# Hybrid convolution/RWKV-7/MLA block on one core: pace of the first three triangular inversions and the distance between their blocks' loads and merges

## The chip, the core and the metric

The kernel runs on one core of a Trainium2 chip: TensorE (PE) multiplies into PSUM, VectorE (DVE) and ScalarE (ACT) work on SBUF and PSUM, GpSimd (POOL) and SyncE (SP) issue most of the DMAs. Each engine takes its own instructions strictly in order and waits on semaphores of the others. The metric is device microseconds (us) from launch to end; lower is better.

## The reference, cut to what matters

Two layers on 1024 latent and 256 context tokens of width 1024. The first layer mixes a short convolution with an RWKV-7 recurrence in 8 heads of 64, run forward and backward; the second is multi-head attention with low-rank keys and queries.

```python
def rwkv7_scan(r, decay, k, v, a_vec, b_vec, s0, reverse):
    def step(S, inp):
        r_t, w_t, k_t, v_t, a_t, b_t = inp
        sa = jnp.einsum('bhij,bhj->bhi', S, a_t)
        S = S * w_t[:, :, None, :] + sa[..., None] * b_t[:, :, None, :] + v_t[..., None] * k_t[:, :, None, :]
        return S, jnp.einsum('bhij,bhj->bhi', S, r_t)
    ...
def even_mixer(...):
    p_all = (h_ctx @ w_in, h_lat @ w_in)
    streams = [rwkv_prep(p[..., A_COLS:A_COLS + RWKV_SHIFT_COLS], mu, k_k) for p in p_all]
    for d, reverse in enumerate((False, True)):
        ...
            decay, k_dir, b_vec = rwkv_direction(k, wl, al, kk, w0[d], w2[d], a0[d], a2[d], k_a)
            y, state = rwkv7_scan(r, decay, k_dir, v, -kk, b_vec, state, reverse)
    ...
```

The kernel does the recurrence in 20 chunks of 64 tokens. Inside a chunk the dependence of each step on those before it is a unit triangular 64x64 matrix, and its inverse is needed for every chunk, head and direction before the scan over chunks can start.

## The kernel before

**The stage.** The change lies in the first layer, in the stretch from about 180 to 720 us of the span. There four kinds of work run interleaved:

- the *chain*: the projections of the first layer (`project`, line 444, 24 matmuls of 128x512 or 128x256 for each part of the 1280 tokens), with what follows them (convolution, gates, shifts);
- the *units*: head pairs j = 0..3 times five groups q of four chunks. A unit (`unit`) makes decays, operands and, for each direction d, the chunk products (`chunks`: line 702 multiplies into PSUM, line 705 masks them on DVE into `M`, whose parts SP sends to HBM, among them the triangular blocks in `g2_d`);
- the *inversion* `invert(j)` of head pair j, which starts when the five units of j are done, so it runs beside the units of j + 1. The inversion of j = 3 has no units left beside it and has an order of its own;
- slices of the second layer's modulation vectors (`ada`, lines 168 to 181).

**The inversion, in steps.** `invert` is a generator, and each `yield` ends a step. Step 1 loads the 32x32 diagonal blocks of both directions (`BL`, line 753, eight DMAs). Steps 2 to 31 are the substitution on DVE (lines 760 and 762, `tm` and `BL`, two instructions a step). Step 32 copies the transposed blocks (`BT`, line 767) and writes both to HBM (`bi_d`, `bt_d`, lines 768 and 769). Then, for each direction d, `blocks(d)` loads them back in the layout that PE wants: `NQ` (line 782, the off-diagonal block from `g2_d`), `X` (line 783, from `bt_d`) and `W` (line 785, from `bi_d`). Some steps pass with nothing in them, and then come the *merges*: two half products of `NQ` and `X` (line 799, 20 instructions of 32x32 each, copied by ACT into the free rows of `NQ` at line 802) and two half products of `NQ` and `W` (line 809, copied by ACT into `W` at line 812), one half a step. The last step of a direction sends `W` to HBM (line 817). For j < 3 all these DMAs are issued by POOL, for j = 3 by SP. `X` and `NQ` have one buffer each, so the loads of d = 1 wait for the merges of d = 0.

**What sets the order.** Only PE's order is the one in which the code is written (`manual_schedule(engines={ET.PE})`); the order of DVE, ACT, POOL and SP is made by the framework's scheduler from priorities and its own estimates. After each of the four parts of a unit (a *quarter*) the code calls `step(rate)`, which advances the chain by `rate` steps and the running inversion by `INV` steps. So `INV` and the empty steps decide after which quarter, and so at which place among PE's instructions, a merge stands. A unit has four quarters, a head pair 20. What is left of an inversion after 20 quarters is written at once (`advance(inv, 99)`).

Of the kernel before, what the change touches and what calls it, by code (L numbers as in the profile page):

```python
# [51 lines left out]
def build(ctx, tc, I, out, dbg=None):  # L52
# [464 lines left out]
    with ExitStack() as c1:  # L517
# [92 lines left out]
                ready.add(j)  # L610
            yield

        RATE, INV, TAIL = ((1.25, 1.75, 1.65, 1.55), (2.2, 0.7, 1.5, 1.4), (1.5, 1.1, 1.3, 2.1), (1.7, 1.5, 0.8, 1.5)), 2.5, (0.5, 1.2)
        INVM = {ET.PE, ET.DVE}
        PAUSE = (3, 0)
        cs = ExitStack()
# [118 lines left out]
        def merge(j):  # L735
            turn[0] += 1
            if j == 3 and turn[0] % 2:
                t = psa.tile([P, 2, 2 * P], F32, tag="A", name="m").rearrange("p a b -> p (a b)")
            elif turn[0] % 2:
                t = psm.tile([P, 512], F32, tag="m", name="m")  # L740
            else:
                t = psb.tile([P, 512], F32, tag="b", name="m")
            return t[:, 0:320].rearrange("p (u t) -> p u t", t=32)

        def invert(j):

            eng = G if j < 3 else SY
            BL = vp.tile([4 * NCH, 2, 32, 32], F32, tag="vA", name="BL")
            for d in range(2):
                for h in range(2):  # L750
                    for b in range(2):
                        p0, r0 = (2 * d + h) * NCH, b * 32
                        eng.dma_start(out=BL[p0:p0 + NCH, b], in_=g2_d[d][:, h, r0:r0 + 32, j, r0:r0 + 32])
            tm = vp.tile([4 * NCH, 32 * 32], F32, tag="vB", name="tm")
            yield
            for q in range(1, 31):
                m = 31 - q
                tgt = BL[:, :, 0:q, q + 1:32]
                tv = tm[:, 0:2 * q * m].rearrange("p (b k i) -> p b k i", b=2, i=m)
                V.tensor_tensor(tv, BL[:, :, q:q + 1, q + 1:32].broadcast_to([4 * NCH, 2, q, m]),  # L760
                                BL[:, :, 0:q, q:q + 1].broadcast_to([4 * NCH, 2, q, m]), op=ALU.mult)
                V.tensor_tensor(tgt, tgt, tv, op=ALU.add)
                yield
            for b in range(2):
                G.memset(BL[:, b].rearrange("p a b -> p (a b)")[:, 0:1024:33], 1.0)
            BT = vp.tile([4 * NCH, 32, 32], F32, tag="vB", name="BT")
            V.tensor_copy(BT, BL[:, 0].rearrange("p s t -> p t s"))
            eng.dma_start(out=bi_d[j].rearrange("d h u b s t -> (d h u) b s t"), in_=BL)
            eng.dma_start(out=bt_d[j].rearrange("d h u s t -> (d h u) s t"), in_=BT)
            yield  # L770
            rows = [(slice(h * 64, h * 64 + 32), slice(h * 64 + 32, h * 64 + 64)) for h in range(2)]
            halves = (slice(0, 10), slice(10, 20))

            def blocks(d):
                W = vp.tile([P, NCH, C], F32, tag=("vA", "vB")[d], name="W")
                if d and j == 3:

                    X, NQ = (vp2.tile([P, NCH, 32], F32, name=n) for n in ("X", "NQ"))
                else:
                    X, NQ = (vp.tile([P, NCH, 32], F32, tag=t, name=t) for t in ("X", "NQ"))  # L780
                for h, (rl, rh) in enumerate(rows):
                    eng.dma_start(out=NQ[rl], in_=g2_d[d][:, h, 0:32, j, 32:64].rearrange("u s t -> s u t"))
                    eng.dma_start(out=X[rl], in_=bt_d[j][d, h].rearrange("u s t -> s u t"))
                    for b, rb in enumerate((rl, rh)):
                        eng.dma_start(out=W[rb, :, b * 32:b * 32 + 32], in_=bi_d[j][d, h, :, b].rearrange("u s t -> s u t"))
                    G.memset(W[rh, :, 0:32], 0.0)
                return W, X, NQ

            ahead = [blocks(d) for d in range(2)] if j == 3 else []
            for d in range(2):  # L790
                W, X, NQ = ahead[d] if ahead else blocks(d)
                for _ in range((6, 3)[d] if j < 3 else PAUSE[d]):
                    yield
                for i, us in enumerate(halves):
                    ps = merge(j)

                    for u in range(10):
                        for rl, rh in rows:
                            TE.matmul(ps[rh, u, :], NQ[rl, us.start + u, :], X[rl, us.start + u, :], start=True, stop=True,
                                      tile_position=(rl.start, rh.start))  # L800
                    for rl, rh in rows:
                        S.copy(NQ[rh, us], ps[rh])
                    if i or j < 3:
                        yield
                for i, us in enumerate(halves):
                    ps = merge(j)
                    for u in range(10):
                        for rl, rh in rows:
                            TE.matmul(ps[rl, u, :], NQ[rh, us.start + u, :], W[rh, us.start + u, 32:64], start=True, stop=True,
                                      tile_position=(rh.start, rl.start))  # L810
                    for rl, rh in rows:
                        S.copy(W[rl, us, 32:64], ps[rl])
                    if j < 3:
                        yield
                if j < 3:
                    for h in range(2):
                        eng.dma_start(out=g1_d[d].rearrange("c p j h x w -> p c j h x w")[hs[h], :, j, h, 3], in_=W[hs[h]])
                else:
                    last_w.append(W)
                yield  # L820
# [50 lines left out]
        for n, (j, q) in enumerate(uo):  # L871
            decays, operands, chunks, bonus = us[n]
            after = us[n + 1]
            if q == 4:
                need(j + 1)
            if q == 2 and j < 3:
                load_w2(j + 1)
            if q == 4 and j < 3:
                split_w2()
            if after:  # L880
                load_x(*uo[n + 1])
            operands(0)
            step(RATE[j][0])
            operands(1)
            if after:
                after[0](0)
            step(RATE[j][1])
            chunks(0)
            if after:
                after[0](1)  # L890
            step(RATE[j][2])
            chunks(1)
            bonus()
            step(RATE[j][3])
            if q == 4:
                advance(inv, 99)
                inv = invert(j)
# [836 lines left out]
```

## Time and profile before

| | us |
|---|---|
| median of 3 runs | 1842.94 |
| lowest, highest | 1842.92, 1848.52 |
| the profiled execution, its own time | 1844.97 |
| span of the profiled execution | 1843.2 |

The span runs from the first to the last instruction of the profiled execution; the rest of its time lies around it. The rows further down come from that one execution. A timeline row gives start, duration, engine, line, operation and tiles, with the idle time of the engine before it and what ended it in brackets; one matmul instruction of the program can leave two records (the products of 32x32 blocks do: 20 instructions, 40 records).

### The profile page before, as it was taken

To read this page: it belongs to the slowest core of one execution; us is meant where nothing else is said; L and a number is where in the kernel's file an instruction comes from. 1 tells how busy PE (TensorE), PEld (TensorE's weight loads), DVE (VectorE), ACT (ScalarE), POOL (GpSimd) and SP (SyncE) were. 2 spreads that over 40 slices of the span, in tenths; PEclk is the share of its full clock that TensorE was granted. 3 is DMA by queue.
4 is the path that set the end of the run, shared out by engine and by line. 5 is a ranking of instruction groups with operands and counts; after the bars stand their busy time and mean duration, and the time that the engine had idled before them with its cause. 6 is when DMAs were issued, how large, how long until landed. Compare 5 with 4: busy or idle time off the path is not lost.

```text
span 1843.2 us, 36929 instructions
## 1 busy us (share of the span) xinstructions
PE 1699.0 (92%) x14352; PEld 1468.0 (80%) x14352; DVE 1206.3 (65%) x2705; ACT 920.1 (50%) x2333; POOL 199.8 (11%) x231
## 2 busy tenths in 40 slices
PE   4999999999999789875899999989999999999999
PEld 3778887878788678775899877878888888888787
DVE  5747579569669283546488563377786886877822
ACT  5747446565544214555244432276666666666610
POOL 1200010320310200100333100000010010010000
PEclk9999999999999989998999999999999999999999
DMA  9067896997987847998544321210010010001242
GB/s 341 26 189 210 224 217 173 282 243 205 247 206 183 190 148 221 325 325 289 166 145 147 101 69 57 88 31 15 18 40 15 22 35 15 21 18 44 95 143 97
DMA packets 243551, 259.37 MB, mean 141 GB/s; under 512 B 67696, under 2 KB 210416, under 8 KB 236912
## 3 DMA queue, kind: packets, MB, share of 16 engines
q1 hardware_dynamic: 188928, 197.39, 35.7%
q10 hardware_dynamic: 48304, 43.52, 8.2%
q0 software_dynamic: 6144, 16.10, 3.8%
q8 instruction: 113, 1.85, 0.4%
q14 instruction: 62, 0.51, 0.1%
HBM read 164.90 MB, written 92.01 MB: 139 GB/s over the span
## 4 chain that ended last, share of the span: by engine, by line
PE 32%; DVE 12%; ACT 5%; issue 1%; DMA 1%; POOL 0%; SPq 0%; ACTq 0%; DVEq 0%; POOLq 0%
PE p L268 8%; PE s_ps L1498 5%; PE o L268 5%; PE o L1191 3%; PE po L1537 3%; PE pk L268 3%; DVE mx L1501 2%; DVE pL L148 2%; PE pT L1525 2%; ACT jk L1448 1%; PE r_ps L1498 1%; ACT p L1510 1%; ACT pH L147 1%; DMA ro<-oz_d 1%; PE pq L268 1%
## 5 line engine op out<-in xcount | busy, mean ns | idle before, releaser
L444 PE MATMUL p<-h0H,wh 128*128 128x512 f32 x744 | 276.4, 372 | 8.8 <-DVE th L458 8.8
L444 PE MATMUL p<-h0H,wl 128*128 128x512 f32 x744 | 267.3, 359 | 0.0
L444 PE MATMUL p<-h0L,wh 128*128 128x512 f32 x744 | 267.1, 359 | 0.0
L444 PEld LDWEIGHTS p<-h0H,wh 128*128 128x128 f32 x744 | 141.9, 191 | 32.3 <-DVE th L458 9.0
L444 PEld LDWEIGHTS p<-h0H,wl 128*128 128x128 f32 x744 | 141.7, 190 | 22.1
L444 PEld LDWEIGHTS p<-h0L,wh 128*128 128x128 f32 x744 | 142.0, 191 | 19.3
L147 ACT CAST pH<-pT 128x512 fp32r<-128x512 f32 x160 | 94.2, 589 | 75.3 <-PE pT L1525 73.4
L148 DVE TENSOR_TENSOR pL<-pT,pH 128x512 fp32r<-128x512 f32 x160 | 109.7, 686 | 30.7 <-ACT pH L147 29.6
L1498 PE MATMUL s_ps<-kH,q 128*128 128x512 f32 x256 | 108.2, 423 | 0.0
L1525 PE MATMUL pT<-cst,p 128*128 128x128 f32 x640 | 98.1, 275 | 10.1 <-DVE mx L1507 3.5
L1501 DVE TENSOR_REDUCE mx<-s_ps 128x1 f32<-128x512 f32 x128 | 87.7, 685 | 22.6 <-PE s_ps L1498 22.1
L1537 PE MATMUL po<-pL,vH 128*128 128x256 f32 x320 | 93.0, 291 | 6.1 <-DVE pL L148 5.3
L1537 PE MATMUL po<-pH,vH 128*128 128x256 f32 x320 | 95.9, 300 | 0.1
L1191 PE MATMUL o<-mh,woH 128*128 128x256 f32 x320 | 92.1, 288 | 1.2 <-DVE y L1082 1.2
L1525 PEld LDWEIGHTS pT<-cst,p 128*128 128x128 f32 x640 | 74.0, 140 | 23.2 <-DVE pL L148 6.3
L1191 PE MATMUL o<-ml,woH 128*128 128x256 f32 x320 | 90.4, 283 | 0.3 <-DVE ml L148 0.3
L1537 PE MATMUL po<-pH,vL 128*128 128x256 f32 x320 | 90.3, 282 | 0.0
L1191 PE MATMUL o<-mh,woL 128*128 128x256 f32 x320 | 90.3, 282 | 0.0
L1510 ACT ACTIVATE p<-s_ps,mx 128x512 f32<-128x512 f32 x128 | 87.6, 692 | 0.1
L1498 PE MATMUL s_ps<-kr,q 128*128 128x512 f32 x256 | 80.6, 396 | 0.2 <-DVE q L1483 0.2
L268 PE MATMUL p<-h1H,w1h 128*128 128x512 f32 x200 | 79.6, 398 | 0.7 <-ACT acc L1292 0.7
L268 PE MATMUL p<-h1H,w1l 128*128 128x512 f32 x200 | 78.0, 390 | 0.0
(346 smaller groups left out, 4584.9 us busy)
## 6 DMA issues: line engine op xcount, KB each, us to landing
G<-g_d SPq DMA_DIRECT2D x40, 1024.0 KB, 8.0
adaw<-in_ada_w_dram ACTq DMA_DIRECT2D x32, 512.0 KB, 5.2
wr<-in_w_in_dram ACTq DMA_DIRECT2D x31, 512.0 KB, 4.1
g_d<-M SPq DMA_DIRECT2D x80, 192.0 KB, 4.4
x<-rkv_d ACTq DMA_DIRECT2D x20, 512.0 KB, 4.6
g_d<-AR SPq DMA_DIRECT2D x80, 128.0 KB, 3.5
g_d<-M SPq DMA_DIRECT2D x80, 128.0 KB, 4.7
adaw<-in_ada_w_dram SPq DMA_DIRECT2D x8, 1024.0 KB, 13.5
```

The lines of the kernel that those rows point to most:

```text
L147: S.copy(H, x)
L148: eng.tensor_tensor(L, x, f(H), op=ALU.subtract)
L268: TE.matmul(ps, w(kt), x(kt), start=q == 0, stop=q == 3 * n - 1)
L444: TE.matmul(ps[:, :n1 - n0], w[:, kt, :], h[:, kt, n0:n1], start=kt + e == 0, stop=kt + e == KT + 1)
L1191: TE.matmul(ps[m // 2][:, m % 2], w[m][:, 4 * e + kt, :], y[:, kt, :], start=e + m % 2 + kt + i == 0, stop=e + m % 2 + kt + i == 7)
L1448: S.activation(jk[:, :b - a], raw[:, i, a:b], AF.Square, accum_out=ss[:, i, e:e + 1])
L1498: TE.matmul(s, x, y[:, n0:n1], start=e == 0, stop=e == 4)
L1501: V.tensor_reduce(mxs[i][:, b:b + 1], s, axis=mybir.AxisListType.X, op=ALU.max)
L1510: S.activation(pt[:, n0:n1], s_ps[i][e - 1] if e else r_ps[:, i, :], AF.Exp, bias=mx[:, 4:5], accum_out=mx[:, 5 + e:6 + e])
L1525: TE.transpose(ps[:, e, i * P:(i + 1) * P], pts[h, n, i][:, (2 * k + e) * P:(2 * k + e + 1) * P], ident)
L1537: TE.matmul(o, a[:, 2 * k + e, :], b[:, e, :], start=k + e + q_ == 0, stop=k + e + q_ == 7)
```

## The change

Two numbers change. Empty steps between the loads and the merges of the first three inversions: nine and five for the two directions instead of six and three. Steps of the inversion a quarter: 2.9 instead of 2.5. The number of instructions of the kernel's work is the same.

```diff
-        RATE, INV, TAIL = ((1.25, 1.75, 1.65, 1.55), (2.2, 0.7, 1.5, 1.4), (1.5, 1.1, 1.3, 2.1), (1.7, 1.5, 0.8, 1.5)), 2.5, (0.5, 1.2)
+        RATE, INV, TAIL = ((1.25, 1.75, 1.65, 1.55), (2.2, 0.7, 1.5, 1.4), (1.5, 1.1, 1.3, 2.1), (1.7, 1.5, 0.8, 1.5)), 2.9, (0.5, 1.2)
...
-                for _ in range((6, 3)[d] if j < 3 else PAUSE[d]):
+                for _ in range((9, 5)[d] if j < 3 else PAUSE[d]):
                     yield
```

By the count of steps, in quarters after the inversion's start:

| step | before | now |
|---|---|---|
| `BT` copied and written | 13 | 11 |
| loads for d = 0 | 14 | 12 |
| first products (line 799), d = 0 | 16 | 15 |
| second products (line 809), first half, d = 0 | 17 | 15 |
| loads for d = 1 | 18 | 16 |
| first products, d = 1, first and second half | 19, 20 | 18, 18 |
| second products, d = 1 | 20 | 19 |
| last step | 21 | 20 |

Where the merges of the second inversion (j = 1) for d = 0 stand among PE's instructions, before (a chunk product of the units at line 702 stands behind the slice at line 176, and the first products come 24 projection matmuls and one slice later):

```order
L444 MATMUL p<-h0H,wl 128x512
L176 MATMUL ada_pt_5084<-cst,adae 128x2
L702 MATMUL A<-AR,BK 128x128 x8
L709 MATMUL b<-cst,BK 128x128 x4
L727 MATMUL b<-x,cst 128x256
```

and now:

```order
L444 MATMUL p<-h0H,wl 128x512
L176 MATMUL ada_pt_5084<-cst,adae 128x2
L799 MATMUL m<-X,NQ 32x32 x40
L809 MATMUL m<-W,NQ 32x32 x20
L702 MATMUL A<-AR,BK 128x128 x8
L709 MATMUL b<-cst,BK 128x128 x4
L727 MATMUL b<-x,cst 128x256
```

Both halves of the first products and one half of the second have moved ahead of the chunk product. The first (j = 0) and the third inversion (j = 2) have the same three rows at the same kind of place, ahead of the second chunk product of the fourth unit.

DVE at the end of the same inversion, before (`BT` is the 652nd of its instructions):

```order
L760 TENSOR_TENSOR tm<-BL 80x60
L682 TENSOR_TENSOR bk<-bk,x 128x4x64
L762 TENSOR_TENSOR BL<-BL,tm 80x2x30
L685 TENSOR_TENSOR BK<-bk,t_4779 128x4x64
L767 COPY BT<-BL 80x1024
L686 TENSOR_TENSOR BK<-bk,t_4779 128x4x64
```

and now:

```order
L760 TENSOR_TENSOR tm<-BL 80x60
L685 TENSOR_TENSOR BK<-bk,t_4787 128x4x64
L762 TENSOR_TENSOR BL<-BL,tm 80x2x30
L686 TENSOR_TENSOR BK<-bk,t_4787 128x4x64
L767 COPY BT<-BL 80x1024
L178 TENSOR_TENSOR ada_109<-ada_pt_4928,vec 128x2
```

Here the copy of `BT` has moved back by one instruction of the units (line 686). In the third inversion it has moved ahead of three (lines 679, 680 and 681), in the first ahead of thirteen.

PE around the last chunk product of the last unit of j = 3, before (the merges are those of the third inversion, d = 1):

```order
L799 MATMUL m<-X,NQ 32x32 x20
L702 MATMUL A<-AR,BK 128x128 x8
L709 MATMUL b<-cst,BK 128x128 x4
L727 MATMUL b<-x,cst 128x256
L444 MATMUL p<-h0H,wh 128x512
```

and now:

```order
L809 MATMUL m<-W,NQ 32x32 x40
L702 MATMUL A<-AR,BK 128x128 x8
L709 MATMUL b<-cst,BK 128x128 x4
L727 MATMUL b<-x,cst 128x256
L444 MATMUL p<-h0H,wh 128x512
```

Before, the other half of the first products and both second products stood twelve projection matmuls behind this chunk product; now all merges stand ahead of it.

## Rows read from the trace of the kernel before

**Rows 1.** The page: busy time of the engines, then PE in forty slices of the span.

```profile
PE 1699.0 (92%) x14352; PEld 1468.0 (80%) x14352; DVE 1206.3 (65%) x2705; ACT 920.1 (50%) x2333; POOL 199.8 (11%) x231
...
PE   4999999999999789875899999989999999999999
```

**Rows 2.** PE's waits from 180 to 720 us: total, times, longest.

```profile
PE p L444 <- DVE th L458: 8.8, 1, 8.8
...
PE m L809 <- ACT NQ L802: 0.4, 2, 0.2
```

**Rows 3.** Timeline of PE: first products that waited, inversions one to three.

```profile
376.14 0.54 PE L799 MATMUL m<-X,NQ 32*32 32x32 f32 x22 [0.51 <-DMA NQ<-g_d]
...
502.30 0.81 PE L799 MATMUL m<-X,NQ 32*32 32x32 f32 x38 [2.11 <-DMA NQ<-g_d]
...
602.36 0.24 PE L799 MATMUL m<-X,NQ 32*32 32x32 f32 x2 [0.37 <-DMA X<-bt_d]
603.54 1.45 PE L799 MATMUL m<-X,NQ 32*32 32x32 f32 x78 [0.94 <-DMA X<-bt_d]
...
622.26 0.22 PE L799 MATMUL m<-X,NQ 32*32 32x32 f32 x2 [2.62 <-DMA NQ<-g_d]
625.57 1.24 PE L799 MATMUL m<-X,NQ 32*32 32x32 f32 x38 [3.09 <-DMA X<-bt_d]
```

**Rows 4.** Timeline of PE: the chunk products ahead of which the merges now stand.

```profile
340.00 1.16 PE L702 MATMUL A<-AR,BK 64*128 64x128 f32 x16
...
473.68 1.16 PE L702 MATMUL A<-AR,BK 64*128 64x128 f32 x16
...
593.64 1.75 PE L702 MATMUL A<-AR,BK 64*128 64x128 f32 x16 [0.76 <-DVE M L705]
```

**Rows 5.** Busy time of PE, PEld, DVE, ACT, POOL; clock, DMA: second and third substitution.

```profile
407.00:461.70 54.70, 53.61 (x377) 44.26 (x377) 53.82 (x112) 26.11 (x62) 0.23 (x2) 1.00 0.79 221
536.00:588.60 52.60, 52.33 (x342) 44.22 (x342) 51.58 (x113) 20.92 (x51) 0.23 (x2) 1.00 0.70 171
```

**Rows 6.** Timeline of DVE: two of the thirteen instructions, and the copies of `BT`.

```profile
321.64 0.47 DVE L562 SCALAR_TENSOR_TENSOR ea<-ea,dv,eb 128x256 f32<-128x256 f32 x1
...
330.64 0.42 DVE L685 TENSOR_TENSOR BK<-bk,t 128x256 f32<-128x256 f32 x1
330.98 1.11 DVE L767 COPY BT<-BL 80x1024 f32<-80x1024 f32 x1
...
461.75 1.13 DVE L767 COPY BT<-BL 80x1024 f32<-80x1024 f32 x1
...
588.61 1.06 DVE L767 COPY BT<-BL 80x1024 f32<-80x1024 f32 x1
```

**Rows 7.** Line 783 in the second inversion: duration, first and last start; issue to landing.

```profile
L783 POOL DMA_DIRECT2D X<-bt_d x2: 682/688/694, 469.6 to 471.6; - x2
...
DMA to landing us min/median/max: 6.8/6.8/6.8
```

**Rows 8.** Line 783's issue-to-landing times over all inversions.

```profile
DMA to landing us min/median/max: 2.6/3.6/6.8
```

**Rows 9.** The end of the units: PE, DVE and PE, from their timelines.

```profile
626.74 2.08 PE L702 MATMUL A<-AR,BK 64*128 64x128 f32 x16
...
649.82 0.22 DVE L760 TENSOR_TENSOR tm<-BL 80x60 f32<-80x60 f32 x1 [18.65 <-DMA X<-v_d]
...
650.94 0.80 PE L444 MATMUL p<-h0H,wh 128*128 128x512 f32 x1 [8.75 <-DVE th L458]
```

**Rows 10.** Stretches, columns as in rows 5: three at the lower clock, one after a wait.

```profile
351.40:358.20 6.80, 6.80 (x84) 6.56 (x76) 0.00 (x0) 1.73 (x5) 3.33 (x5) 0.50 1.03 292
...
500.00:524.00 24.00, 21.89 (x283) 18.57 (x283) 10.75 (x23) 11.09 (x27) 9.79 (x12) 1.00 0.98 245
...
624.40:631.30 6.90, 5.73 (x62) 5.17 (x63) 1.71 (x3) 1.42 (x3) 0.00 (x0) 0.51 0.85 200
...
645.00:655.20 10.20, 4.26 (x10) 3.39 (x11) 5.04 (x15) 0.00 (x0) 0.00 (x0) 0.50 0.83 221
```

## The prediction, on record before the changed kernel ran

> **What bounds the kernel now.** First the page: PE is busy 92% of the span, and most of its forty slices show 9 or more [rows 1], so an edit counts where it makes PE wait. Then PE's waits in the stage of the change, 180 to 720 us: the longest single one is 8.8 us for DVE at line 458 [rows 2]. Then the timeline of PE at line 799, the first products of the merges: six waits for loads, 0.51 in the first inversion, 2.11 in the second, 0.37, 0.94, 2.62 and 3.09 in the third, 9.6 us in all [rows 3]. These are what a longer distance between loads and merges can take away. Against them stand the places to which the merges move [rows 4], and whether their data can be there by then, which DVE decides: during the substitution it is busy 53.8 of 54.7 us in the second inversion and 51.6 of 52.6 in the third [rows 5].
>
> **The change part by part.**
>
> *The pace, 2.9 for 2.5.* By the count of steps `BT` is written two quarters sooner. But the count orders PE alone. DVE takes the substitution between the units' instructions in an order of its own, and it is full [rows 5]: its order puts `BT` behind one more instruction of the units in the second inversion, ahead of three in the third, ahead of thirteen in the first. An instruction of those costs some 0.42 us less 0.08 of overlap. So `BT` comes 0.4 us later in the second, 1.0 sooner in the third; in the first the thirteen, from 321.64 to 330.64, make 6.8 us sooner [rows 6]. It is not two quarters: from `BT` to `BT`, 461.75 to 588.61, are 20 quarters, 6.3 us each, so two would be 12.7 us.
>
> *From `BT` to `X`.* In the second inversion `BT` is done at 462.88 [rows 6]; the loads of `X` are issued at 469.6 and 471.6 and land 6.8 us later, at 476.4 and 478.4 [rows 7], 13.5 and 15.5 us behind `BT`. In the third `BT` is done at 589.67 and the products start when `X` lands, at 603.54 [rows 3, 6]: 13.9 us.
>
> *Second inversion, d = 0.* The first products now stand ahead of the chunk product that started at 473.68 [rows 4]. `X` lands between 476.4 and 478.4, plus 0.4. The wait is 2.7 to 5.1 us; I take 4.1, near the middle.
>
> *Third inversion, d = 0.* PE reached the chunk product at 593.64 - 0.76 = 592.88 and waited 0.76 for DVE [rows 4]. Now it meets the first products there, whose `X` lands at 603.54 - 1.0 = 602.5: a wait of 9.7, of which 0.76 was there already. 8.9 more, 7.9 to 9.9 with a microsecond for the DMAs either way.
>
> *First inversion, d = 0.* `BT` done at 332.09 - 6.8 = 325.3, `X` 13.9 to 15.5 later, at 339.2 to 340.8, against PE at 340.00 [rows 4]. The last load of `W` follows `X`'s second by two issues of 0.69 [rows 7], as long as the first products take (1.45 us [rows 3]). Together 0 to 1.6; I take 0.8.
>
> *Second products directly behind the first, at three places.* They need ACT's copies of the first half. The nearest row is 0.2 us at most, where this happened before [rows 2]; three times, 0.6. If ACT is in something longer, 1.5. What stands behind a waiting merge on PE is the chunk product, and behind the copies on ACT the units' other evictions, which wait for the same PE work; I add nothing for them.
>
> *The waits that were.* For d = 1 the loads are issued two quarters ahead of the first products instead of one, some 6 us more than the 0.51, 2.11 and 2.62 + 3.09 us that they were late. These go, and 0.37 + 0.94 of the third inversion are replaced by the wait above: -9.6. In the third inversion the merges of d = 0 are themselves so late that `NQ` may still come late: 0 to 2.6, as before; I take 1.0.
>
> *Merges that pass the last chunk product.* Before, one half of the first products and both second products of the third inversion, d = 1, stood behind it. Now they stand ahead: 0.7 + 1.5 us of the shape in rows 3, 2.2. They cost nothing on PE as such. But from that chunk product (626.74) runs the chain to the last inversion: mask, SP's writes, SP's loads of `BL`, first substitution at 649.82, and line 458 behind it, for which PE then stood 8.75 us and went on at 650.94 [rows 9]. That wait swallows nothing, since its end moves with the chunk product. What follows (the rest of the projections, the last merges, the scan) moves with it.
>
> *The clock.* Three stretches of 6.8 to 10.2 us stand at 1.2 instead of 2.4 GHz. PE is busy in them for 6.80, 5.73 and 4.26 us, and loses half of that: 3.4, 2.9, 2.1. The second lies behind the 2.62 and 3.09 us waits, the third in the 8.75 us one; after the 2.11 us wait the clock stayed at 1.00 [rows 9, 10]. The second should go: -2.9. The new waits of 4.1 and 9.7 us should bring one each: 2.0 (0 to 3.4) and 2.1 (as behind the 8.75). Sum 1.2, from -2.9 to 4.5.
>
> **Sum.** 4.1 + 8.9 + 0.8 + 0.6 - 9.6 + 1.0 + 2.2 + 1.2 = 9.2 us. On the profiled execution's own 1844.97 that is 1854.2. The median of the runs shown lies 2.0 below it, so I predict 1852. With all terms at their ends the sum goes from about 0.7 to 17.8, that is 1843.6 to 1860.7 against the median.
>
> **The rivals.**
>
> *The loads land sooner.* Over all inversions `X` took from 2.6 us [rows 8]. With 2.6 instead of 6.8 in the second inversion its wait is gone with the clock's 2.0; a load about 1.0 sooner takes as much off the third: 9.2 - 4.1 - 2.0 - 1.0 = 2.1, some 1845, no change to be measured. For it: the DMAs will be in other company. Against it: the path from `BT` to `X` was 13.5 to 15.5 us in the second and 13.9 in the third.
>
> The Trainium skill, page "DMA: Bandwidth & Descriptors", section "Anatomy of one DMA — SWDGE (gpsimd) path", says that a DMA from GpSimd takes about 2.0 us plus its bytes by 436 GB/s; for a load of 80 KB that is 2.2 us, by my estimate. With such times for writes and loads the second inversion would not wait at all and the third some 6 us less, and the sum would be about -4, some 1839. The trace does not agree: `X` took 6.8 us [rows 7].
>
> *The last inversion does not move.* If the first substitution at 649.82 hangs on a transfer that has nothing to do with the last chunk product, PE's delay (9.2 - 2.2 = 7.0) is swallowed in its 8.75 us wait: no change, 1843. For it: the row names a load of `X` from `v_d` as what came last [rows 9]. Against it: `BL` needs the last chunk's blocks, and SP issues that load behind those of `BL`, so both come with the chunk.
>
> *The substitution really ends two quarters sooner.* It is the other side. If DVE gave the inversion its place by the count, `X` would come 12.7 us sooner, ahead of PE in the second and third inversion. Then no merge of d = 0 waits; 9.6 and the clock's 2.9 are saved, 2.2 is paid: -10.3, about 1833. It decides from a lead of 9.7 us in the third inversion. Against it: rows 5, and the order of DVE's instructions, which is the order in which they run. This is also how the change would do what its numbers say. I see no slack on DVE for it.
>
> **How the numbers follow.** About 0.3% (5.5 us) can be told from no change. The forecast has 0.68, the sooner loads 0.12, the last inversion that stays 0.11, the sooner substitution 0.09. Slower by over 0.3%: 0.68, nearly all of the forecast, and a little more for loads that land later than I have them: 0.69. Within: 0.22. Faster: 0.09. The range from 1843 to 1861 takes in the ends of the sum and the two cases without a change, and leaves out the sooner substitution and what lies beyond the ends.
>
> **What will show it.** In the changed kernel's timeline of PE: at line 799 a wait for `X` of about 4 us in the second inversion (near 475) and of 9 to 10 in the third (near 597), and none over 1 us for d = 1 but perhaps in the third. `BT` within 1.5 us of 461.75 and of 588.61, shifted by what PE has lost by then, and near 324 in the first. Line 809 directly behind line 799 with 0.2 to 0.5 us. The wait for line 458 longer than 8.75 us by about 2, and ending near 660. A stretch at 1.2 GHz at each long wait, and none behind d = 1 of the third. I am wrong if `BT` in the third inversion comes more than 5 us before 588, if PE's wait there is under 5 us, or if the first substitution of the last inversion stays near 650.

## Result and profile of the changed kernel

| | before | after |
|---|---|---|
| median, us (runs) | 1845.73 (4) | 1878.22 (4) |
| lowest, highest | 1842.92, 1852.95 | 1870.61, 1881.44 |
| profiled execution, us | 1844.97 | 1870.61 |
| its span | 1843.2 | 1868.8 |

The change makes the kernel slower: ratio 1.0161, 95% interval 1.0131 to 1.0192, some 30 us (the two medians lie 32.5 apart). The prediction had the direction, but 9 us, and its range ended at 1861. The profiled execution of after is the fastest of its four, so its trace shows 26 of the 30 us.

The page of after, busy time and PE in forty slices (answers to [rows 1]): PE's share fell by a point, and the slice with the first inversion's merges, 327 to 374 us, shows 8 where 9 stood.

```profile
PE 1704.9 (91%) x14352; PEld 1473.1 (79%) x14352; DVE 1206.5 (65%) x2705; ACT 918.2 (49%) x2333; POOL 200.6 (11%) x231
...
PE   4999999899899779777799999989999999999999
```

PE's waits in after, from 180 to 745 us: what was waited for, total, times, longest (answers to [rows 2]). The waits for `NQ` are gone; in their place stand `X`, a longer wait for line 458, and others that the prediction did not have or had smaller: at lines 653, 809 and 799 for ACT, at line 168 for the weights of the slices (`adaw`).

```profile
PE m L799 <- DMA X<-bt_d: 14.5, 4, 8.6
PE p L444 <- DVE th L458: 13.9, 1, 13.9
PE b L653 <- ACT t L656: 2.3, 1, 2.3
PE ada_ps L168 <- DMA adaw<-in_ada_w_dram: 2.1, 1, 2.1
...
PE m L809 <- ACT NQ L802: 1.9, 2, 1.7
...
PE m L799 <- ACT M L710: 1.0, 1, 1.0
```

PE's timeline in after at the new places of the merges, first, second and third inversion (answers to [rows 3, 4]; the brackets hold the idle time before a row and what ended it):

```profile
340.96 0.39 PE L653 MATMUL b<-wl,w2h 128*128 128x256 f32 x1 [2.34 <-ACT t L656]
...
346.60 0.80 PE L168 MATMUL ada_ps<-adaw,scp 128*32 128x128 f32 x16 [2.14 <-DMA adaw<-in_ada_w_dram]
348.38 2.42 PE L799 MATMUL m<-X,NQ 32*32 32x32 f32 x80 [0.98 <-ACT M L710]
352.47 1.71 PE L809 MATMUL m<-W,NQ 32*32 32x32 f32 x40 [1.67 <-ACT NQ L802]
...
485.47 0.24 PE L799 MATMUL m<-X,NQ 32*32 32x32 f32 x2 [3.55 <-DMA X<-bt_d]
486.84 2.32 PE L799 MATMUL m<-X,NQ 32*32 32x32 f32 x78 [1.13 <-DMA X<-bt_d]
...
618.70 0.31 PE L799 MATMUL m<-X,NQ 32*32 32x32 f32 x2 [8.58 <-DMA X<-bt_d]
620.25 2.34 PE L799 MATMUL m<-X,NQ 32*32 32x32 f32 x78 [1.24 <-DMA X<-bt_d]
```

In the second and third inversion PE waits for `X`, 4.7 and 9.8 us, as forecast. In the first it does not wait for `X` at all, but 7.1 us for other things.

Stretches of after at the lower clock (columns as in rows 5; answers to [rows 10]): the granted clock is 0.50, that is 1.2 GHz, in five stretches. PE is busy in them for 28.71 us; by the prediction's reckoning it loses half of that, 14.4, against half of 16.8, 8.4, in the three of before.

```profile
347.00:357.20 10.20, 7.42 (x152) 6.46 (x142) 6.95 (x14) 8.21 (x24) 3.29 (x5) 0.50 0.90 254
486.90:493.70 6.80, 6.80 (x141) 6.42 (x141) 1.29 (x2) 2.80 (x7) 3.96 (x6) 0.50 0.38 95
548.30:551.70 3.40, 3.40 (x11) 2.74 (x10) 2.58 (x7) 2.56 (x6) 0.00 (x0) 0.51 1.02 265
613.20:626.90 13.70, 6.96 (x141) 6.54 (x142) 4.41 (x11) 3.62 (x11) 8.56 (x13) 0.50 0.63 173
664.40:678.10 13.70, 4.13 (x10) 3.26 (x11) 4.94 (x14) 0.00 (x0) 0.00 (x0) 0.50 0.82 182
```

Where the time goes shows best in the delay of equal work. The projection matmuls (line 444) are the same, in the same order, in all kernels here; the table gives how much later one of them starts than in before, less the same difference at 181 us (the executions come there some 3 us apart, with equal work behind them).

| PE in before at, us | 308 | 404 | 517 | 545 | 590 | 600 | 640 | 652 | 700 |
|---|---|---|---|---|---|---|---|---|---|
| what lies just ahead of it | | 1st inversion | 2nd, merges | behind them | 3rd, substitution | 3rd, d = 0 | 3rd, d = 1 | wait, L458 | |
| after | 0.5 | 5.4 | 11.2 | 14.6 | 15.3 | 29.9 | 15.9 | 21.1 | 21.0 |
| first_only | 0.8 | 9.2 | 14.8 | 14.8 | 15.1 | 15.6 | 12.2 | 11.4 | 11.4 |
| second_only | 0.0 | -1.5 | 3.8 | 7.9 | 8.5 | 8.0 | 7.1 | 4.2 | 3.9 |
| third_only | 0.0 | -3.4 | -0.7 | -0.7 | -0.4 | 12.9 | 0.1 | 4.2 | 3.9 |
| second_and_third | 0.0 | -1.7 | 2.8 | 7.9 | 7.6 | 22.4 | 8.4 | 12.8 | 13.1 |

(The lower four rows are from the experiments.) One execution is good to 3 or 4 us: at 404, where the last three have only run what before runs, they stand at -1.5 to -3.4. There before itself is slow: its lower clock lasts from 351.4 to 358.2 us [rows 10], 6.8 us; in third_only and second_and_third it lasts 3.4 at this place, in second_only it does not fall. So the ratios carry the verdicts, and the traces tell the place.

### The profile page after: what moved, and what is told of

Same layout as the page of the kernel before. It is cut to its first block, busy times and chain, and to the rows that moved or that the text cites. A ratio compares the mean times of both kernels' runs of the same rounds, so it can differ in the third digit from the quotient of the medians.

```text
span 1868.8 us, 36926 instructions
## 1 busy us (share of the span) xinstructions
PE 1704.9 (91%) x14352; PEld 1473.1 (79%) x14352; DVE 1206.5 (65%) x2705; ACT 918.2 (49%) x2333; POOL 200.6 (11%) x231
## 4 chain that ended last, share of the span: by engine, by line
PE 30%; DVE 12%; ACT 5%; DMA 2%; issue 1%; POOL 1%; SPq 0%; ACTq 0%; DVEq 0%; POOLq 0%
PE p L268 8%; PE s_ps L1498 5%; PE o L268 5%; PE po L1537 3%; PE pk L268 3%; PE o L1191 2%; DVE mx L1501 2%; DVE pL L148 2%; PE pT L1525 2%; ACT jk L1448 1%; PE r_ps L1498 1%; ACT p L1510 1%; DMA ro<-oz_d 1%; ACT pH L147 1%; DMA gn<-mix_d 1%
## 5 line engine op out<-in xcount | busy, mean ns | idle before, releaser
L444 PE MATMUL p<-h0H,wh 128*128 128x512 f32 x744 | 275.3, 370 | 15.7 <-DVE th L458 13.9
```

The source lines that it names most:

```text
L444: TE.matmul(ps[:, :n1 - n0], w[:, kt, :], h[:, kt, n0:n1], start=kt + e == 0, stop=kt + e == KT + 1)
```

## Experiments: the three inversions apart

In all of these the pace and the empty steps are given for each inversion; the rest is the kernel before. In first_only the first inversion has the numbers of the change (the second number of `PACE` is the count carried over from the units ahead):

```diff
-        PAUSE = (3, 0)
+        PAUSE, PACE, PAUSES = (3, 0), ((2.9, 0.9999), (2.5, 0.0), (2.5, 0.0)), ((9, 5), (6, 3), (6, 3))
...
-                for _ in range((6, 3)[d] if j < 3 else PAUSE[d]):
+                for _ in range(PAUSES[j][d] if j < 3 else PAUSE[d]):
...
-            paced += INV
+            paced += pace
...
-                inv = invert(j)
+                inv, (pace, paced) = invert(j), PACE[min(j, 2)]
```

> The change in the first inversion alone (2.9 steps a quarter, nine and five empty steps for j = 0; the second and third inversions as in the kernel before). The prediction's terms for the first inversion: a wait for X of 0.8 us, 0.2 for ACT's copies, less the old 0.51 us wait: +0.5 us, no difference that can be measured. The rival, from the delay of equal projection matmuls between the two traces (2.5 us at 308, 8.2 us at 437 in the trace before): the substitution on DVE, moved ahead of thirteen instructions of the units, holds up what PE needs, first of all the weights split at line 148, whose buffer the next load waits for: +5.7 us, with a new wait of about 2.3 us at line 653 near 341, one of about 2 at line 168 near 347 and a half-clock stretch of about 10 us behind them.

Measured: ratio 1.0071 (1.0053 to 1.0088), some 13 us. The forecast's 0.5 us is refuted, and the rival's 5.7 is too small as well, though its waits at lines 653 and 168 are there. PE's waits in first_only, 310 to 400 us, columns as above; in before the longest wait there is 1.3 us.

```profile
PE b L653 <- ACT t L656: 2.7, 1, 2.7
PE m L809 <- ACT NQ L802: 2.6, 1, 2.6
...
PE m L799 <- ACT M L710: 1.3, 1, 1.3
PE ada_ps L168 <- DMA adaw<-in_ada_w_dram: 1.0, 1, 1.0
PE ada_pt L176 <- ACT adae L172: 1.0, 1, 1.0
```

For second_only and third_only the values move to the other inversions:

```diff
+ second_only: PACE, PAUSES = ((2.5, 0.0), (2.9, 0.9999), (2.5, 0.0)), ((6, 3), (9, 5), (6, 3))
+ third_only:  PACE, PAUSES = ((2.5, 0.0), (2.5, 0.0), (2.9, 0.9999)), ((6, 3), (6, 3), (9, 5))
+ second_and_third: PACE, PAUSES = ((2.5, 0.0), (2.9, 0.9999), (2.9, 0.9999)), ((6, 3), (9, 5), (9, 5))
```

> The change in the second inversion alone. The prediction's terms: X +4.1, ACT's copies +0.2, the old wait of 2.11 gone, a half-clock stretch +2.0: +4.2 us. The delay of equal matmuls between the traces (8.2 us at 437, 13.2 us at 517) says +5.1. Both expect a wait at line 799, d = 0, of 4 to 5 us near 474, none at d = 1. If the second inversion cost much more or less than 4 to 5 us, what the first had done to the state of the queues would be part of it.

Measured: 1.0042 (1.0025 to 1.0059), 7.7 us.

> The change in the third inversion alone. The prediction's terms: X +8.9, ACT's copies +0.2, NQ of d = 1 +1.0, half clock +2.1 - 2.9, the merges that pass the last chunk product +2.2, old waits of 0.37, 0.94, 2.62 and 3.09 gone: +4.5 us. The delay of equal matmuls between the traces (13.2 us at 517, 17.3 at 576, 18.0 at 636, 23.0 at 651, 25.7 in the scan) says more: +4.0 during the third substitution, +0.8 over the merges, +5.0 up to the last inversion, some 2.6 in the scan, 10 to 12 us. Both expect a wait for X of 9 to 10 us near 593.

Measured: 1.0038 (1.0023 to 1.0054), 7.0 us. The expectations of 4.2 and 4.5 us lie at the lower ends of these intervals or just outside them; the 10 to 12 us that the delays of equal work said for the third are too much.

> The change without its part in the first inversion. If the parts add up: 0.42 + 0.38 = 0.8% more than before, some 15 us, and the first inversion's 0.71% is what is missing to the whole change (1.61%). The prediction's terms for the second and third inversion give 8.7 us, 0.47%. If the lateness of the first inversion makes the others dearer, it is clearly less than 0.8%.

Measured: 1.0081 (1.0064 to 1.0098), 14.9 us. The parts add up: 0.81 + 0.71 = 1.52% against 1.61% for the whole. PE's waits in second_and_third from 430 to 680 us:

```profile
PE p L444 <- DVE th L458: 13.1, 1, 13.1
PE m L799 <- DMA X<-bt_d: 12.7, 4, 8.3
PE ada_ps L168 <- DMA adaw<-in_ada_w_dram: 3.7, 1, 3.7
```

`X` has 12.7 us here, where the forecast had 13.8. What it did not have: 3.7 us at line 168 (533.63 us) for weights of the modulation slices, with 3.4 us at the lower clock behind it. In second_only and in after there stand, a chunk product later, 0.78 us for `M` and 3.4 us at the lower clock. This is the step from 517 to 545 us in the table: 3.4 to 5.1 us in the three kernels that move the second inversion's merges, and nothing in the two that don't.

**Pace without the new places.** Thirteen empty steps for d = 0 keep the merges in their old quarters at the new pace:

```diff
+ second_pace_alone: PACE, PAUSES = ((2.5, 0.0), (2.9, 0.9999), (2.5, 0.0)), ((6, 3), (13, 5), (6, 3))
+ third_pace_alone:  PACE, PAUSES = ((2.5, 0.0), (2.5, 0.0), (2.9, 0.9999)), ((6, 3), (6, 3), (13, 5))
```

> In the second inversion alone 2.9 steps a quarter, but thirteen and five empty steps, so that its merges stay where the kernel before has them. If what the change costs there (0.42% in second_only) is the wait for X at the merges' new place, with the half clock behind it: no difference to the kernel before (within 0.15%), the waits for NQ at line 799, d = 1, as before. If it is the earlier substitution, as a part of the first inversion's cost was: 0.2 to 0.4% more.

> The same for the third inversion: 2.9 steps a quarter with thirteen and five empty steps, merges where they were. If the 0.38% of third_only come from the wait for X and from the last chunk product that the merges hold up: no difference to the kernel before (within 0.15%), the wait at line 458 some 9 us. If the earlier substitution costs: 0.2 to 0.4% more.

Measured: 0.9990 (0.9975 to 1.0004) and 0.9991 (0.9978 to 1.0003). In the second and third inversion the pace costs nothing that can be measured; what they cost hangs on the merges' new places.

**The distance of d = 1 alone.**

```diff
+ d1_later: PACE, PAUSES = ((2.5, 0.0), (2.5, 0.0), (2.5, 0.0)), ((6, 5), (6, 5), (6, 5))
```

> The other way to lengthen the distance: the pace of before (2.5), six and five empty steps for all three inversions, so that the merges of d = 0 stay where they were, and those of d = 1 move behind the last quarter of the units instead of coming sooner. If the waits of d = 1 (0.51, 2.11, 2.62 and 3.09 us) and the half-clock stretch behind the last two (2.9) are really to be had by distance alone, the time falls by up to 11 us, and the merges of the third inversion go into the time in which PE stood 8.75 us before the last inversion. If the last merges then hold up the scan instead, or the loads only land later, no change.

Measured: 1.0021 (1.0007 to 1.0035). The waits of d = 1 are gone, and still nothing is won. PE's waits in d1_later from 360 to 680 us:

```profile
PE p L444 <- DVE th L458: 14.3, 1, 14.3
PE m L809 <- ACT NQ L802: 4.8, 2, 4.6
```

The last inversion's start on DVE, from its timeline in d1_later, and there the writes of `W` (line 817: duration, first and last start). In before the first is at 649.82 [rows 9], the last write at 638.2.

```profile
654.89 0.22 DVE L760 TENSOR_TENSOR tm<-BL 80x60 f32<-80x60 f32 x1 [21.01 <-DMA X<-v_d]
```

```profile
L817 POOL DMA_DIRECT2D g_d<-W x4: 899/908/915, 618.3 to 643.8; - x4
```

`tm` of the last inversion takes the buffer of that `W`, so later merges can hold it up; the loads of `BL` came later too (last issue 650.1 us, before 645.4), and the two were not told apart.

## Experiments: the first inversion

The trace names a chain. DVE's order puts the end of the substitution ahead of thirteen instructions, and line 148 is one of them: it splits a block of the projections' weights. DVE's timeline in after; in before line 148 stood at 325.09, ahead of `BT` at 330.98 [rows 6]:

```profile
326.26 1.11 DVE L767 COPY BT<-BL 80x1024 f32<-80x1024 f32 x1
...
328.89 1.20 DVE L148 TENSOR_TENSOR wl<-wr,wh 128x1024 fp32r<-128x1024 f32 x1
```

Its buffer `wr` then takes the next load, on ACT's queue. ACT's timeline in before and in after (line 253 issues the load, line 147 is the cast that uses it, line 656 stands behind the cast, and PE's line 653 waits for line 656):

```profile
326.34 0.34 ACTq L253 DMA_DIRECT2D wr<-in_w_in_dram  x1
...
332.86 1.05 ACT L147 CAST wh<-wr 128x1024 fp32r<-128x1024 f32 x1 [4.50 <-DMA wr<-in_w_in_dram]
```

```profile
330.12 0.33 ACTq L253 DMA_DIRECT2D wr<-in_w_in_dram  x1
331.65 0.60 ACTq L625 DMA_DIRECT2D x<-rkv_d  x1
...
332.40 2.69 ACTq L159 DMA_DIRECT2D adaw<-in_ada_w_dram  x1
...
338.85 1.04 ACT L147 CAST wh<-wr 128x1024 fp32r<-128x1024 f32 x1 [5.80 <-DMA wr<-in_w_in_dram]
...
340.06 0.84 ACT L656 ACTIVATE t<-b,dv 128x256 f32<-128x256 f32 x2
```

The load is issued 3.8 us later and used 6.0 later; the slices' weights (`adaw`), issued behind it, come when PE has waited 2.14 us. Then the merges meet an ACT that is behind: 0.98 and 1.67 us. The first edit gives the split a priority that puts it ahead again:

```diff
-            if x == 0:
-                fetched()
+            with tc.high_priority(200) if len(order) == 16 else ExitStack():
+                fetched() if x == 0 else None
```

> As first_only, but one split of the projections' weights (lines 147 and 148, whose end lets the next load of weights, line 253, start) is given a higher priority, so that it stands ahead of the end of the substitution on DVE again, and its cast earlier on ACT. PE's order is that of first_only. If the 13 us of first_only (0.71%) come from this split, which the substitution had passed: the load of the weights is issued some 8 us sooner, the waits of 2.65 us at line 653 and 1.0 at line 168 and the half clock behind them go, and the time falls to within 5 us of the kernel before. If they come from the merges' new places or from the loads of the inversion beside the units', it stays at 10 to 13 us more than before.

Measured: 1.0051 (1.0032 to 1.0070). The wait at line 653 is gone, as the chain has it; but 9 us stay, where within 5 were expected, and the interval overlaps that of first_only. The priority did more than put the load back: line 253 issues it at 318.19 us, even ahead of before (326.34). PE, 310 to 400 us, now waits at the merges instead:

```profile
PE m L799 <- ACT M L710: 3.1, 1, 3.1
...
PE m L799 <- DMA W<-bi_d: 1.4, 1, 1.4
PE ada_ps L168 <- DMA adaw<-in_ada_w_dram: 1.3, 2, 0.9
```

> The control: the kernel before with the same priority for the same split. There no long wait of PE near 340 goes back to that load, so no difference that can be measured (between -2 and +2 us); if it gains as much as first_split_ahead gains against first_only, the split is only a help anywhere and not the cause.

Measured: 0.9995 (0.9978 to 1.0011). The priority by itself is worth nothing.

```diff
+ first_pace_alone: PACE, PAUSES = ((2.9, 0.9999), (2.5, 0.0), (2.5, 0.0)), ((13, 5), (6, 3), (6, 3))
```

> In the first inversion 2.9 steps a quarter as in the change, but thirteen and five empty steps, so that its merges stay where the kernel before has them (quarters 16, 17 and 19, 20); substitution, copy of BT, its writes and the loads of d = 0 come sooner as in first_only. If what the substitution passes on DVE is the cause: line 653 waits for ACT as in first_only (2 to 3 us) and the total is 5 to 13 us more than before. If the merges' places are the cause: no difference to the kernel before.

Measured: 1.0040 (1.0023 to 1.0056). By difference the new places are some 0.3% of the 0.71 and the pace 0.4, each uncertain by some 0.2. Here the pace costs, unlike in the second and third inversion. PE waits at lines 653 and 168 as expected of the weights' chain:

```profile
PE ada_ps L168 <- DMA adaw<-in_ada_w_dram: 4.2, 1, 4.2
PE b L653 <- ACT t L656: 2.0, 1, 2.0
```

```diff
+ first_substitution_alone: PACE as in first_pace_alone, PAUSES = ((7, 5), (6, 3), (6, 3))
                 V.tensor_tensor(tgt, tgt, tv, op=ALU.add)
-                yield
+                yield from [None] * ((1, 7)[q == 30] if j == 0 else 1)
```

> As first_pace_alone, but six of the empty steps stand between the end of the substitution and the copy of BT, which is then taken 8 instructions of DVE later, and with it the 960 KB of writes to HBM. The substitution itself still passes the split of the weights. If the late issue of the weights' load alone is the cause, the wait at line 653 stays at 2 to 3 us; if the load is slow because the inversion's writes run beside it (8.7 us from issue to the cast against 6.5 before), it shrinks by some 2 us. Total between 0 and 8 us more than before.

Measured: 1.0021 (1.0007 to 1.0035), which overlaps the interval of first_pace_alone. No wait at line 653, 2.7 us at line 168. Only the write of `BT` came later (332.37 us); that of `BL`, two thirds of the bytes, was issued at 326.70 as before the edit, so this run does not separate writes from order.

```diff
+ first_pace_split: the pace and empty steps of first_pace_alone, and the priority of first_split_ahead
```

> The first inversion with 2.9 steps a quarter, its merges where the kernel before has them (thirteen and five empty steps), and the split of the weights with the higher priority: first_pace_alone and first_split_ahead in one. If these two are the causes: 0.1% or less above the kernel before (first_pace_alone had 0.40%), no wait at line 653 and little at line 168. If the earlier loads and writes of the inversion beside those of the projections' weights are a cause of their own: 0.2 to 0.4% stay, with a wait at line 168 for the slices' weights.

Measured: 1.0037 (1.0018 to 1.0055). The trace has no wait at line 653, 1.5 us at line 168 and 1.4 at line 702; the time is no better than first_pace_alone's. So the theory of two causes, split and places, falls: with both away, most of the pace's cost stays (the interval begins at 0.18%, and 0.1 or less was expected).

```diff
-            eng.dma_start(out=bi_d[j].rearrange("d h u b s t -> (d h u) b s t"), in_=BL)
+            if j: eng.dma_start(out=bi_d[j].rearrange("d h u b s t -> (d h u) b s t"), in_=BL)
...
-                        ... in_=bi_d[j][d, h, :, b].rearrange("u s t -> s u t"))
+                        ... in_=(bi_d[j][d, h, :, b] if j else bt_d[j][d, h]).rearrange("u s t -> s u t"))
```

> first_pace_alone without the write of BL to HBM in the first inversion (line 768, 640 KB; left out: the loads of W then read BT's blocks, so the merges of the first inversion compute with other numbers). If the load of the slices' weights comes late because the inversion's writes run beside it: the wait at line 168 near 344 shrinks from 4.2 us to under 1.5, line 653's stays near 2, and the total falls from 0.40% to 0.2% or less above the kernel before. If the write has nothing to do with it: 4 us at line 168 and 0.4% stay.

> The control: the kernel before without the same write (left out in the same way). PE waits there for no load near 340, so no difference that can be measured; what it gains is to be taken off what first_pace_fewer_writes gains.

Measured: 1.0005 (0.9992 to 1.0018), and the control 0.9963 (0.9951 to 0.9975). The first number alone would have named the write as the cause. The control takes it back: without the write the kernel before gains as much, so between the two the pace still costs 0.42%. PE's wait at line 168 stays as well (4.4 us), and the wait at line 653, which was to stay near 2, is gone without a gain. The write is not what the change costs. The next suspects, the loads of `X` and `W` and the other instructions passed on DVE, were not tried one by one.

**What stays open.** Of the first inversion's 0.71%, about 0.3 goes with the merges' places. The 0.4 of the pace shows in the trace as waits at lines 653 and 168, but taking the first away gave nothing back in first_pace_split. Which passed instruction or which load costs it was not settled. The traces go one step further. In all seven kernels with the new pace in the first inversion ACT stops ahead of the next load of weights (line 253), and line 662, which stands behind that load, starts after 3.45 to 7.68 us of idle time. With the old pace it is 0.55 to 0.96 us in ten kernels and 3.36 in second_only. ACT's timeline in before, first_pace_alone and first_pace_split:

```profile
336.11 0.60 ACT L662 ACTIVATE bk<-t,dv 128x256 f32<-128x256 f32 x1 [0.57 <-DMA adaw<-in_ada_w_dram]
...
345.06 0.60 ACT L662 ACTIVATE bk<-t,dv 128x256 f32<-128x256 f32 x1 [4.07 <-DMA g_d<-M]
...
346.53 0.60 ACT L662 ACTIVATE bk<-t,dv 128x256 f32<-128x256 f32 x1 [7.68 <-DMA adaw<-in_ada_w_dram]
```

In first_pace_split the stop is longer and ends no sooner, which fits that removing the wait at line 653 gave nothing back. A transfer ends it, by the traces the slices' weights or a write of the units. No run moves that transfer alone, so this is the place of the cost and not yet its cause.

## Experiments: two versions that are not slower

```diff
-        owed = 0.0
+        owed = 2.0
         for n, _ in enumerate(inv):
```

> The kernel before, with two steps of the projections moved ahead of the first step of the last inversion's substitution (the count that paces them starts at 2 instead of 0), so that PE has work in the 8.75 us in which it waits for line 458. If that wait is lost time: 5 to 8 us less. If DVE's substitution sets the end of that stage, and PE's wait is only its slack, as the prediction's term for the last chunk product says (what delays the chunk product delays everything behind): within 2 us of before, with the wait gone and PE waiting later instead.

Measured: 0.9970 (0.9959 to 0.9981), 5.5 us less than before: faster than both kernels. PE's waits in last_ahead_2 from 630 to 715 us; the 8.8 us for line 458 are gone, 3.9 come later:

```profile
PE p L444 <- DVE g L483: 2.2, 2, 1.2
PE m L809 <- issue: 1.7, 1, 1.7
```

So most of that wait was lost time. The substitution began at 648.58 there, no later than in before (649.82): the wait's end did not move, PE and DVE only had work up to it.

```diff
+ kept_places_last_ahead: PACE, PAUSES = ((2.5, 0.0), (2.9, 0.9999), (2.9, 0.9999)), ((6, 3), (13, 5), (13, 5))
+ and owed = 2.0 as above
```

> Second and third inversion with 2.9 steps a quarter and thirteen and five empty steps, so that their merges stay in their old places; the first as before; and two steps of the projections ahead of the last inversion's first step, as in last_ahead_2. If the pace alone costs nothing there and the last change is worth what it was alone (0.3%): 0.3 to 0.5% less than before, some 1840 us. If the two pace changes hold each other up: no better than last_ahead_2, or worse.

Measured: 0.9977 (0.9959 to 0.9994). The two paces together don't hurt and don't add: it is last_ahead_2 within the interval.

## Why the prediction was too small

| term | forecast, us | after, by its trace and the runs |
|---|---|---|
| second inversion, `X` | 4.1 | 3.55 + 1.13 = 4.7 |
| third inversion, `X` | 9.7 in all | 8.58 + 1.24 = 9.8 |
| waits of d = 1 | all gone, 1.0 left | all gone, none left |
| first inversion, `X` | 0.8 | 0; 7.1 of other waits; 13 in first_only |
| ACT's copies | 0.6 | 1.9, nearly all in the first inversion |
| behind a waiting merge | 0 | none; but 3.4 to 5.1 from 517 to 545 us, behind a transfer |
| last chunk product passed | 2.2 | wait 13.88 instead of 8.75 |
| clock | +1.2 | +6.0 (14.4 against 8.4), from one execution each |

**What held.** Both waits for `X`, to 0.6 us, and by their working: from the end of the copy of `BT` in the second inversion (472.22, below) to PE's two rows behind `X` (485.47, 486.84) are 13.3 and 14.6 us, against 13.5 and 15.5 forecast; in the third (606.09 to 618.70 and 620.25) 12.6 and 14.2 against 13.9. In second_only and second_and_third the second's wait was 3.2 and 3.0 us. In after it came so close partly by luck: `X` was issued 8.0 us behind `BT` instead of 6.7 and landed in 5.2 us at most instead of 6.8, and the two differences cancel. `BT` moved on DVE as said: 9.4 us later in the second (PE had lost 8.2), 16.4 in the third (17.2), and in the first it came at 326.26, 4.7 sooner (PE had lost 2.4). From DVE's timeline in after:

```profile
471.12 1.10 DVE L767 COPY BT<-BL 80x1024 f32<-80x1024 f32 x1
...
605.02 1.07 DVE L767 COPY BT<-BL 80x1024 f32<-80x1024 f32 x1
```

So the rival of a sooner substitution is out. So is that of a last inversion that stays: it began at 672.85 instead of 649.82. The loads of `X` did land sooner, but they were issued later, so the waits stayed and that rival's time did not come. The Trainium skill, page "DMA: Bandwidth & Descriptors", section "Anatomy of one DMA — SWDGE (gpsimd) path", would again have had 2.2 us for a load of `X` (an estimate from its formula); the trace has 4.6 to 5.2 for the four that PE waited for.

**First step that failed: the first inversion.** The prediction counted the thirteen passed instructions as 6.8 us that `BT` gains, and did not ask who waits for the thirteen. Line 148 is among them; behind it hang a load on ACT's queue, the slices' weights issued after it, the cast, line 656, and PE, which the trace shows waiting at lines 653 and 168, where it had not waited. Nor did it ask what ACT would be doing when the merges came. Alone the first inversion cost 0.71%, some 13 us against 0.5 in the sum, nearly half of the whole. Not all of it lies at its own merges: in first_only's trace 9.2 us are lost by 404 and 5.6 more by 517, beside the second inversion. How it divides is open, as said.

**Second: a wait that no term had.** For what is queued behind a waiting merge the prediction said "I add nothing for them", and that held: in after no chunk product right behind a merge waits. What the sum lacked comes later. In the second inversion the step from 517 to 545 us costs 3.4 to 5.1 us, when its merges are done (the last start at 517.32 in after). ACT's line 457 stands idle there for 10.6 to 13.1 us, until transfers land, in the three kernels that move these merges; in all others it waits only for PE, 4.0 us at most. One of the transfers is SP's write of `mix_d` (line 491), which frees a buffer `th` of line 457. From one such write to the next SP takes 18.5 to 22.6 us in the three, 14.7 in before. ACT's and SP's timeline in after:

```profile
539.06 0.60 ACT L457 ACTIVATE th<-p 128x512 f32<-128x512 f32 x1 [10.90 <-DMA adaw<-in_ada_w_dram]
```

```profile
533.88 0.33 SPq L491 DMA_DIRECT2D mix_d<-th  x1
```

Behind line 457 come DVE's line 458 and the mask, and PE waits for the mask or for the slices' weights, 0.78 to 3.72 us, and the clock falls once more. With this step the 4.2 us of the second inversion become about the 7.7 that were measured. That SP is slower because the moved merges write their `W` (line 817) amid SP's writes is likely, not shown: these writes start at 510.5 to 520.0 us there, between the two writes of `mix_d`, and in before behind them.

**Third: a gain booked where there is slack.** The prediction let the lower clock behind the waits of d = 1 go, -2.9, and with it let the wait at line 458 grow by the 2.2 us of merges that moved. But that stretch, 624.4 to 631.3 [rows 10], lay mostly behind the last chunk product (626.74), where PE only runs towards its wait, and the wait's end hangs on the chunk product. PE from the last chunk product to the wait: 15.45 us in before, 10.6 in after, third_only and second_and_third. These 4.8 us, 2.2 of merges and by difference 2.6 of clock, all went into the wait: from the chunk product to its end it is 24.2 us in before and 24.5 in after (20.6 to 22.8 in eleven other kernels with the old places there, 23.4 and 23.7 in third_only and second_and_third, so this holds to some 2 us). So by these traces nearly all of the -2.9 was no gain, and the third inversion's 4.5 becomes some 7, as measured. PE's timeline in after, the last chunk product and the wait behind it:

```profile
649.47 1.16 PE L702 MATMUL A<-AR,BK 64*128 64x128 f32 x16
...
673.97 0.79 PE L444 MATMUL p<-h0H,wh 128*128 128x512 f32 x1 [13.88 <-DVE th L458]
```

The other half of the clock term was short too: at the waits for `X` the lower clock lasted 6.8 and 13.7 us, where the prediction took 2.0 and 2.1 of loss; PE was busy there for 6.80 and 6.96 us, a loss of 3.4 and 3.5.

Together: 0.5 becomes 13, 4.2 becomes 7.7, 4.5 becomes 7; the sum is 28 us, against 30 measured.

## What to carry to other kernels

When a step is moved past others on a full engine, list the others and follow each to whoever waits for it, through the loads and writes that it lets start; the step that moves is the smaller half of the account. A stall that is removed counts only if no wait with a fixed end lies between it and the end of the chain: measure from the event that releases the wait, not from where PE stands. And take an experiment that leaves work out together with the same cut in the kernel before: without the control, a write that costs both kernels the same would have passed for the cause.

## What was not expected of the hardware

Without one write of 640 KB to HBM by POOL's queue in the first inversion, for which PE does not wait, the kernel before took 0.37% (0.25 to 0.49) less, some 7 us (the loads of `W` kept their number and size, but read what `BT`'s write had left; the loads of `X` also started 5.9 us behind the start of `BT`'s copy instead of 9.6). This is in line with the Trainium skill, page "Trainium Kernel Development and Optimization", section "Key Constraints", by which the DMAs of all queues run on the same 16 engines; the runs show only the sum, not which transfer it delays. And one execution does not tell what a short wait does to PE's granted clock. In after it fell to 1.2 GHz from 548.3 to 551.7 us when PE had waited just 0.78 us, for `M` at 545.5, while 2.11 us in before left it at 1.00 [rows 3, 10]. But the same wait, 2.08 and 2.06 us long, in third_only and last_ahead_2 was followed by 3.4 us at 1.2 GHz. So the prediction's reading that the clock holds at such a wait rested on one execution.
